# First modulations of a two-layer diffusion block: alternating weight chunks, shift from unsplit fp32 weights, and conditioning rows prepared at another place

## The chip, the cores and the metric

The kernel runs on one core of a Trainium2 chip. A core has five engines that run side by side, each with its own queue in fixed order: TensorE (PE, matmuls), VectorE (DVE), ScalarE (ACT), GpSimd (POOL) and SyncE (SP), which here only issues DMA transfers. What counts is the time of one execution on the device, in microseconds (us), lower being better.

## The reference, cut to what matters

Two layers of a block that works on 256 latent tokens beside 256 context tokens, 1024 features wide. Each layer begins with a modulation whose shift and scale come from a conditioning vector:

```python
def adaln(cond, w_ada, b_ada):
    return jnp.split(jax.nn.silu(cond) @ w_ada + b_ada, 6, axis=-1)

def modulate(x, shift, scale):
    return rms_norm(x) * (1.0 + scale) + shift

for l in range(DEPTH):
    sh1, sc1, g1, sh2, sc2, g2 = adaln(c, w_ada[l], b_ada[l])          # latent tokens
    csh1, csc1, cg1, csh2, csc2, cg2 = adaln(c_ctx, w_ada[l], b_ada[l])  # context tokens
    ... project(modulate(ctx, csh1, csc1), w_in[l])   # keys, values, gates of the context
    ... project(modulate(x, sh1, sc1), w_in[l])       # three token mixers, merged, w_o
    ... sq_relu_ffn(modulate(x_new, sh2, sc2), w_ff1[l], w_ff2[l])
```

All weights are fp32. `w_ada` is 1024 x 6144 a layer; its first 2048 columns give `sh1` and `sc1` for both conditioning vectors. They are needed before the first projection can start.

## The kernel before, in words

Tokens lie along columns, features along the 128 partitions. A precise product is made of fast passes: a weight chunk arrives as fp32 `raw` (128x1024), ScalarE rounds it to `whi`, VectorE (later in turns with POOL) forms `wlo = raw - whi`, and TensorE adds hi*hi, hi*lo and lo*hi. `emit_chunk` (L284) issues the DMA of a chunk and its split; `chunk` (L301) hands out the next chunk and emits two ahead. The order of all chunks is the list `layer_chunks`, and it begins with `START_ORDER`. Eight `raw` buffers exist at the start (four under the tag `raw`, four under `t4k`), so the DMA of chunk n + 8 waits until chunk n has been read by its split.

The start of the first layer is `start` (L1340). It runs as a main generator beside spawned chains, which a small planner (`run`) lets go on when their due time on its clock is reached (the table `LAT`); that fixes the order of TensorE and SP. The order on VectorE, ScalarE and POOL is set when the program is built. `start` does the following:

- loads `x` for both streams (`xT`, latent and context, 1 MB each), and spawns `norm_start0` (L1284) for each: squares (L1290), sums (L1294, L1295), a matmul with ones, the power -1/2 on POOL (L375), a row of 1/rms spread by two matmuls with `dg` (L519) into `Rb`, and `x*R` (L1304), one half of `x` on VectorE and one on POOL;
- computes the first modulations in four groups of 512 columns, shift and scale of the first half, then of the second (`ada_group`, L1308): the four columns of `csil` (two conditioning vectors, each as hi and lo) are the stationary operand, the split weights move, 512 columns at a time, into a `sc` bank of PSUM. `ada_rows` (L1324) turns the four rows with a small matmul against `comb` to columns and adds the bias;
- `half(i)` (L1354) makes `nt` from scale and shift for four of the eight feature blocks and splits it into `h`;
- kv and q parts of the first projection follow, four of each, `half(1)` needed by the second half of them. Then the constants are loaded (`load_constants2`, `layer_params`), the first kv and q chains are started, and last `cond_rows` (L460) prepares `sil`, the conditioning vectors in every partition, for later `ada_task` products (L490) on VectorE.

The kv chain and the q chain (`qss`, `rq`, `qt` in the rows) follow; TensorE turns `qt` and `KS` by transposes (L320), which stand among its matmuls.

Of the kernel before, what the change touches and what calls it, by code (L numbers as in the profile page):

```python
# [143 lines left out]
def shape_constants():  # L144
# [38 lines left out]
    comb = np.array([[1, 0], [0, 1], [1, 0], [0, 1]], np.float32)  # L183
# [7 lines left out]
       "ada": 1.51, "x": 0.54, "half": 1.35, "kv_lat": 6.0, "kv_ctx": 4.5, "kv_out": 0.7, "q_lat": 7.5,  # L191
# [15 lines left out]
class Builder:  # L207
# [183 lines left out]
    def load_constants(self):  # L391
# [892 lines left out]
    def norm_start0(self, s, x, R):  # L1284
# [11 lines left out]
        yield self.lat("x")  # L1296
# [5 lines left out]
        for i in range(2):  # L1302
            xh = x[:, i * 4:i * 4 + 4, :]
            (nc.vector if i == 0 else nc.gpsimd).tensor_tensor(  # L1304
                xh, xh, R.unsqueeze(1).to_broadcast([P, 4, SEQ]), op=ALU.mult)
        self.flags.add(f"R{s}")

    def ada_group(self, g):  # L1308
        c0 = ADA_START[g]
        ps = self.sc_bank()  # L1310
        for kc in range(4):
            if kc > 0:
                yield
            w = self.chunk(("B", "w_ada", c0, 512, 2 * kc))
            for kk in range(2):
                k = 2 * kc + kk
                for q in range(2):
                    self.mm(ps[:4, :], self.csil[:, k, :], w[q][:, kk * 512:(kk + 1) * 512],
                            start=(k == 0 and q == 0), stop=(k == KT - 1 and q == 1))
        rows = self.tp.tile([4, 512], F32, tag="t2k", name="adarow")  # L1320
        self.nc.scalar.copy(rows, ps[:4, :])
        self.spawn(self.ada_rows(g, rows), self.lat("ada"))

    def ada_rows(self, g, rows):  # L1324

        nc = self.nc
        out = self.sc_bank()
        ov = out[:, :8].rearrange("p (n c) -> p n c", c=2)
        for j in range(4):
            self.mm(ov[:, j, :], rows[:, j * P:(j + 1) * P], self.comb, True, True)  # L1330
# [3 lines left out]
        nc.vector.tensor_tensor(o, ov.rearrange("p n c -> p c n"), b, op=ALU.add)
        if n0 >= 8:
            nc.vector.tensor_scalar(o, o, 1.0, None, op0=ALU.add)
        self.flags.add(f"ada{g}")
        yield 0.0

    def start(self, h, kv_ready, q_ready):  # L1340
# [127 lines left out]
```

## Time and profile before

| | us |
|---|---|
| median of three runs | 1434.76 |
| fastest and slowest | 1433.84, 1438.26 |
| the profiled execution | 1438.17 |
| its span, first to last instruction | 1436.4 |
| TensorE busy | 1366.7 (95%) |
| VectorE busy | 991.7 (69%) |
| ScalarE busy | 661.6 (46%) |
| POOL busy | 451.7 (31%) |

A busy time is the sum of the times in which an engine worked on something; matmuls overlap, so a busy TensorE need not be at its peak. Wait lists name the engine and operation that released the waiting one. The mean granted TensorE clock of the span is 0.979 of full speed. The chain of work that ended last is mostly TensorE (41% of the span) and VectorE (10%).

### The profile page before, as it was taken

Reading aid. Unit: us, or ns where it says so; the run is one execution under the profiler, and the core shown is the slowest. Engines: PE = TensorE matmul, PEld = TensorE weight load, DVE = VectorE, ACT = ScalarE, POOL = GpSimd, SP = SyncE. Lnnn points to the kernel's source line nnn. Section 1 sums busy time; section 2 is a strip of 40 time slices with the busy share of each in tenths; the row PEclk is TensorE's granted clock in tenths of the full one; section 3 lists DMA queues with packets and bytes.
Section 4 is the critical chain, followed back from the end, with each engine's and each line's share of the span. In section 5 each row is a group of like instructions: output and inputs, shape, how many; then the busy total and the mean of one; then the engine's idle time right before and its main releaser. Section 6 shows DMA issues by size and latency. Waiting matters only on the chain.

```text
span 1436.4 us, 21724 instructions
## 1 busy us (share of the span) xinstructions
PE 1366.7 (95%) x8272; PEld 1192.3 (83%) x8272; DVE 991.7 (69%) x1669; ACT 661.6 (46%) x1095; POOL 451.7 (31%) x288
## 2 busy tenths in 40 slices
PE   4968998998999999999999999999999999999999
PEld 2757787877788889888887888987799999999999
DVE  7776678876576768768885566886875665864453
ACT  5755455643223335442332323555556635565443
POOL 2030002213112334553342424431110245465554
PEclk8989999998999999999999999999999999999999
DMA  7621112321354455444556656442144335556554
GB/s 301 230 73 45 59 64 68 118 103 45 118 175 162 150 196 182 158 140 172 205 207 213 216 193 215 165 149 89 48 138 149 104 118 161 180 162 202 181 178 131
DMA packets 60391, 214.08 MB, mean 149 GB/s; under 512 B 7230, under 2 KB 8510, under 8 KB 59648
## 3 DMA queue, kind: packets, MB, share of 16 engines
q1 hardware_dynamic: 58696, 209.51, 43.5%
q10 hardware_dynamic: 1592, 3.20, 0.7%
q8 instruction: 65, 1.06, 0.3%
q14 instruction: 38, 0.31, 0.1%
HBM read 211.63 MB, written 1.05 MB: 148 GB/s over the span
## 4 chain that ended last, share of the span: by engine, by line
PE 41%; DVE 10%; issue 3%; DMA 3%; ACT 1%; POOL 0%; SPq 0%; DVEq 0%; ACTq 0%; POOLq 0%
PE mm L316 37%; DVE junk L490 4%; DMA adaw<-w_adaT 3%; PE sm L316 2%; DVE wlo L298 1%; PE sc L316 1%; PE sm L320 1%; DVE acc L507 1%; ACT whi L296 0%; DVE h L546 0%; DVE x L1259 0%; DVE f L1215 0%; DVE mx L717 0%; DVE nt L541 0%; ACT gab L820 0%
## 5 line engine op out<-in xcount | busy, mean ns | idle before, releaser
L296 ACT CAST whi<-raw 128x1024 fp32r<-128x1024 f32 (+1 forms) x312 | 322.9, 1039 | 524.1 <-PE mm L316 419.0
L316 PE MATMUL mm<-h,whi 128*128 128x512 f32 (+2 forms) x2112 | 515.1, 336 | 1.7 <-ACT h L1177 0.8
L316 PEld LDWEIGHTS mm<-h,whi 128*128 128x128 f32 x2112 | 361.7, 192 | 40.8 <-DVE h L1178 1.1
L298 DVE TENSOR_TENSOR wlo<-raw,whi 128x1024 fp32r<-128x1024 f32 (+1 forms) x215 | 286.7, 1336 | 107.9 <-ACT whi L296 106.7
L316 PE MATMUL mm<-h,wlo 128*128 128x512 f32 (+2 forms) x1056 | 352.4, 334 | 0.0
L298 POOL TENSOR_TENSOR wlo<-raw,whi 128x1024 fp32r<-128x1024 f32 x97 | 240.1, 2475 | 346.7 <-ACT whi L296 340.9
L316 PE MATMUL mm<-f,whi 128*128 128x256 f32 (+1 forms) x1152 | 257.2, 319 | 0.0
L490 DVE SCALAR_TENSOR_TENSOR junk<-adaw,sil 128x1024 bf16<-128x1024 f32 x128 | 184.9, 1472 | 57.0 <-DMA adaw<-w_adaT 56.8
L316 PEld LDWEIGHTS mm<-h,wlo 128*128 128x128 f32 x1056 | 202.2, 192 | 19.2
L316 PEld LDWEIGHTS mm<-f,whi 128*128 128x128 f32 x1152 | 192.0, 191 | 15.2
L316 PE MATMUL mm<-f,wlo 128*128 128x256 f32 (+1 forms) x576 | 183.8, 319 | 2.9 <-DVE wlo L298 2.4
L316 PE MATMUL mm<-whi,h 128*128 128x512 f32 (+2 forms) x544 | 172.0, 386 | 0.0
L316 PEld LDWEIGHTS mm<-f,wlo 128*128 128x128 f32 x576 | 109.7, 190 | 11.7 <-DVE wlo L298 3.7
L316 PEld LDWEIGHTS mm<-whi,h 128*128 128x128 f32 x544 | 103.7, 199 | 16.3
L316 PE MATMUL mm<-wlo,h 128*128 128x512 f32 (+2 forms) x272 | 102.9, 378 | 0.4 <-DVE wlo L298 0.4
L1214 POOL TENSOR_TENSOR ffr<-ffr 128x512 f32<-128x512 f32 (+1 forms) x64 | 71.5, 1118 | 46.1 <-ACT f L1213 37.5
L1215 DVE TENSOR_TENSOR f<-ffr,f 128x512 fp32r<-128x512 f32 (+1 forms) x64 | 56.2, 886 | 29.7 <-POOL ffr L1214 29.5
L1259 DVE SCALAR_TENSOR_TENSOR x<-mm,ada,x 128x256 f32<-128x256 f32 x96 | 43.6, 478 | 42.5 <-PE mm L316 42.3
L383 POOL TENSOR_SCALAR gx<-gx 128x512 f32<-128x512 f32 (+1 forms) x14 | 14.0, 1000 | 183.2 <-ACT gx L382 183.1
L316 PE MATMUL mm<-m,whi 128*128 128x256 f32 x384 | 69.5, 283 | 0.0
L316 PEld LDWEIGHTS mm<-wlo,h 128*128 128x128 f32 x272 | 54.2, 199 | 8.1 <-DVE wlo L298 1.1
L1061 POOL TENSOR_TENSOR mg<-mg,gth 128x512 f32<-128x512 f32 (+1 forms) x28 | 34.4, 1230 | 84.1 <-DVE gth L1060 84.1
(291 smaller groups left out, 1828.5 us busy)
## 6 DMA issues: line engine op xcount, KB each, us to landing
raw<-wpk SPq DMA_DIRECT2D x304, 512.0 KB, 3.8
adaw<-w_adaT SPq DMA_DIRECT2D x80, 512.0 KB, 3.8
raw<-wpk SPq DMA_DIRECT2D x8, 288.0 KB, 2.9
x<-xT SPq DMA_DIRECT2D x2, 1024.0 KB, 6.9
x<-xT ACTq DMA_DIRECT2D x2, 1024.0 KB, 6.9
sil<-cond SPq DMA_DIRECT2D x1, 1024.0 KB
out<-x ACTq DMA_DIRECT2D x8, 128.0 KB, 1.7
trif<-tri SPq DMA_DIRECT2D x2, 384.0 KB, 2.9
```

Of the source, the lines that this page charges most:

```text
L296: nc.scalar.copy(hi[:, :n], raw[:, :n])
L298: eng.tensor_tensor(lo[:, :n], raw[:, :n], hi[:, :n].bitcast(F32), op=ALU.subtract)
L316: self.nc.tensor.matmul(out, lhsT, rhs, start=start, stop=stop)
L320: self.nc.tensor.transpose(out, src, self.ident)
L383: nc.gpsimd.tensor_scalar(x2[:, :n], x2[:, :n], 0.044715, 1.0, op0=ALU.mult, op1=ALU.add)
L490: nc.vector.scalar_tensor_tensor(junk, raw, 1.0, self.sil[:, c], op0=ALU.mult, op1=ALU.mult, accum_out=self.ada[l][:, c, n:n + 1])
L507: nc.vector.tensor_tensor(acc, acc, sq, op=ALU.add)
L1061: (nc.vector if m is not None and n >= KT - 2 else nc.gpsimd).tensor_tensor(mg, mg, th[:, :nt], op=ALU.add)
L1214: nc.gpsimd.tensor_tensor(r[:, :nt], r[:, :nt], r[:, :nt], op=ALU.mult)
L1215: nc.vector.tensor_tensor(lo, r[:, :nt], hi.bitcast(F32), op=ALU.subtract)
L1259: nc.vector.scalar_tensor_tensor(x[s][:, n], ps[:, s * SEQ:(s + 1) * SEQ], self.ada[l][:, s, 40 + n:41 + n], x[s][:, n], op0=ALU.mult, op1 ...
```

## The change

Sixteen chunks of `w_ada` are taken in two halves rather than four groups, shift and scale chunks alternating. Shift chunks (columns below 1024) are no longer split: TensorE reads `raw` itself, with the plain fp32 `cth` (two columns) as the stationary operand, into rows 32 and 33 of a PSUM bank. Scale chunks are split as before, into rows 0 to 3 of another. Both end in one tile `rows` of 34 partitions, which POOL sets to zero first, and `comb` grows to 34x4. The two `x` are issued among the first chunks, and `x*R` moves into `half`, all of it on VectorE. `cond_rows`, `load_constants2` and `layer_params` move ahead of the first kv part, and `cond_rows` works on pieces of 512 columns; its factor 0.5 goes into the accumulating product of `ada_task`. `comb` is loaded later. Four entries of the planner's times change (`ada`, `x`, now one for each stream, `half`, `rstd0`).

```diff
+ADA_START = ((0, 1024), (512, 1536))
-START_ORDER = [("B", "w_ada", c0, 512, kk) for c0 in ADA_START[:2] for kk in range(0, KT, 2)]
-START_ORDER += [("B", "w_ada", c0, 512, kk) for c0 in ADA_START[2:] for kk in range(0, KT, 2)]
+START_ORDER = [("B", "w_ada", c0, 512, kk) for cs in ADA_START for kk in range(0, KT, 2) for c0 in cs]
...
-       "ada": 1.51, "x": 0.54, "half": 1.35, "kv_lat": 6.0, "kv_ctx": 4.5, "kv_out": 0.7, "q_lat": 7.5,
+       "ada": 1.5, "x0": 5.0, "x1": 8.5, "half": 3.0, "kv_lat": 6.0, "kv_ctx": 4.5, "kv_out": 0.7, "q_lat": 7.5,
...
         nc.sync.dma_start(raw[:, :n], src)
+        if self.specs[i][1] == "w_ada" and self.specs[i][2] < D:
+            self.split[i] = raw, None
+            return
...
-        self.csil = self.big([P, KT, 4], F32R, name="csil")
-        self.split_hl(self.csil[:, :, 0:2], self.csil[:, :, 2:4], thv)
+        self.csil = thv
+        self.csil2 = cp.tile([P, KT, 4], F32R, name="csil2")
+        self.split_hl(self.csil2[:, :, 0:2], self.csil2[:, :, 2:4], thv)
...
         for c in range(2):
-            th = self.wp.tile([P, D], F32, tag="raw", bufs=4, name="silt")
-            nc.scalar.activation(th, self.sil[:, c], AF.Tanh, scale=0.5)
-            nc.vector.scalar_tensor_tensor(th, th, 1.0, self.sil[:, c], op0=ALU.add, op1=ALU.mult)
-            nc.vector.tensor_scalar(self.sil[:, c], th, 0.5, None, op0=ALU.mult)
+            for i in range(2):
+                v = self.sil[:, c, i * 512:(i + 1) * 512]
+                th = self.trb(name="silt")
+                nc.scalar.activation(th, v, AF.Tanh, scale=0.5)
+                nc.vector.scalar_tensor_tensor(v, th, 1.0, v, op0=ALU.add, op1=ALU.mult)
...
-        for i in range(2):
-            xh = x[:, i * 4:i * 4 + 4, :]
-            (nc.vector if i == 0 else nc.gpsimd).tensor_tensor(
-                xh, xh, R.unsqueeze(1).to_broadcast([P, 4, SEQ]), op=ALU.mult)
         self.flags.add(f"R{s}")
 
-    def ada_group(self, g):
...
+    def ada_half(self, i):
+
+        nc = self.nc
+        ps = [self.sc_bank() for _ in range(2)]
+        rows = self.tp.tile([34, 512], F32, tag="t2k", name="adarow")
+        nc.gpsimd.memset(rows, 0.0)
         for kc in range(4):
+            for j, c0 in enumerate(ADA_START[i]):
+                w, wl = self.chunk(("B", "w_ada", c0, 512, 2 * kc))
+                for kk in range(2):
+                    k = 2 * kc + kk
+                    c = slice(kk * 512, kk * 512 + 512)
+                    if j == 0:
+                        self.mm(ps[0][32:34], self.csil[:, k], w[:, c], k == 0, k == KT - 1)
+                        self.clk += 0.43
+                    else:
+                        self.mm(ps[1][:4], self.csil2[:, k], w[:, c], k == 0, False)
+                        self.mm(ps[1][:4], self.csil2[:, k], wl[:, c], False, k == KT - 1)
                 yield
+        nc.scalar.copy(rows[32:34], ps[0][32:34])
+        nc.vector.tensor_copy(rows[:4], ps[1][:4])
+        self.spawn(self.ada_rows(i, rows), self.lat("ada"))
...
         for s in range(2):
+            for _ in range(2):
+                self.emit_chunk()
             nc.sync.dma_start(x[s], self.a["xT"][s])
...
         def half(i):
-            yield from self.until(f"ada{2 * i}", f"ada{2 * i + 1}", "R0", "R1")
+            yield from self.until(f"ada{i}", "R0", "R1")
+            for s in range(2):
+                xh = x[s][:, i * 4:i * 4 + 4, :]
+                nc.vector.tensor_tensor(xh, xh, Rs[s].unsqueeze(1).to_broadcast([P, 4, SEQ]), op=ALU.mult)
...
-        self.spawn(half(0), 0.0)
-        yield from ada[2]
-        yield from ada[3]
+        for i in range(2):
+            yield from self.ada_half(i)
+            self.spawn(half(i), 0.0)
+        self.cond_rows()
+        self.load_constants2()
+        self.layer_params(0)
         yield from self.need("half0")
...
-        self.spawn(half(1), 0.0)
...
-        self.load_constants2()
-        self.layer_params(0)
...
-        self.cond_rows()
```

TensorE's first matmuls, before (a row is one instruction or several alike; outputs stand left of the arrow, `csil` and `cth` are the conditioning vectors, `dg` spreads 1/rms):

```order
L316 MATMUL sc<-whi,csil 4x512
L316 MATMUL sc<-wlo,csil 4x512
L316 MATMUL sc<-whi,csil 4x512
L316 MATMUL sc<-wlo,csil 4x512
L316 MATMUL sm<-ones,sq_126 128x1 x2
L316 MATMUL sm<-ones,sq_138 128x1 x2
```

and now:

```order
L321 MATMUL sc<-raw,cth 2x512 x2
L321 MATMUL sc<-whi,csil_105 4x512
L321 MATMUL sc<-wlo,csil_105 4x512
L321 MATMUL sc<-whi,csil_105 4x512
L321 MATMUL sc<-wlo,csil_105 4x512
L321 MATMUL sc<-raw,cth 2x512 x2
```

A shift chunk has become two fp32 matmuls in front of each scale chunk, and the statistics (`sq`) stand further back, behind the fourth chunk for the first stream.

VectorE around `x*R` (the rows `x<-x,Rb`), before:

```order
L519 TENSOR_SCALAR dg<-ident,rn 128x128 x4
L298 TENSOR_TENSOR wlo<-raw,whi 128x1024
L1304 TENSOR_TENSOR x<-x,Rb 128x1024 x2
L298 TENSOR_TENSOR wlo<-raw,whi 128x1024 x3
L1334 TENSOR_TENSOR ada_97<-sc,bada 128x2x4
L298 TENSOR_TENSOR wlo<-raw,whi 128x1024 x4
```

and now:

```order
L527 TENSOR_SCALAR dg<-ident,rn 128x128 x2
L1303 TENSOR_TENSOR sq_154<-sq_154 128x256
L303 TENSOR_TENSOR wlo<-raw,whi 128x1024 x2
L1372 TENSOR_TENSOR x<-x,Rb 128x1024 x2
L379 TENSOR_SCALAR rn<-sm 128x2
L303 TENSOR_TENSOR wlo<-raw,whi 128x1024
L1332 COPY adarow<-sc 4x512
L527 TENSOR_SCALAR dg<-ident,rn 128x128 x2
L303 TENSOR_TENSOR wlo<-raw,whi 128x1024
L1372 TENSOR_TENSOR x<-x,Rb 128x1024 x2
L1348 TENSOR_TENSOR ada_95<-sm,bada 128x2x4
```

The first halves of both `x` are scaled on VectorE, two instructions for each stream, with splits between them, and the split count ahead of `ada` is smaller.

VectorE in the first q chain (`qss` is the sum of squares of a head, `rq` its power's input, `silt` and `sil` the conditioning rows), before:

```order
L468 SCALAR_TENSOR_TENSOR silt<-silt,sil 128x1024
L627 TENSOR_TENSOR KS<-kvz,KS 128x2x64 x2
L622 TENSOR_TENSOR kvz<-kvz,parb 128x128
L469 TENSOR_SCALAR sil<-silt 128x1024
L298 TENSOR_TENSOR wlo<-raw,whi 128x1024
L665 TENSOR_REDUCE qss<-qt_701 128x8
L627 TENSOR_TENSOR KS<-kvz,KS 128x2x64 x2
L468 SCALAR_TENSOR_TENSOR silt<-silt,sil 128x1024
L374 TENSOR_SCALAR rq<-qss 128x8
```

and now:

```order
L673 TENSOR_REDUCE qss<-qt_655 128x8
L630 TENSOR_TENSOR kvz<-kvz,parb 128x128
L379 TENSOR_SCALAR rq<-qss 128x8
L303 TENSOR_TENSOR wlo<-raw,whi 128x1024
L635 TENSOR_TENSOR KS<-kvz,KS 128x2x64 x2
L676 TENSOR_TENSOR Q_119<-Q_119,rq 128x512
L303 TENSOR_TENSOR wlo<-raw,whi 128x1024
L680 TENSOR_TENSOR Q_119<-Q_119,parb 128x512
L303 TENSOR_TENSOR wlo<-raw,whi 128x1024
L685 TENSOR_TENSOR qt_655<-Q_119,qt_655 128x4x64
```

The conditioning rows are gone from here (they stand ahead of the second half's `ada` now), and two splits have come between the steps that end in `qt`.

## Rows read from the trace of the kernel before

**Rows 1.** Busy us by stretch: PE, PEld, DVE, ACT, POOL; granted clock, DMA share, GB/s

```profile
0.00:4.00 4.00, 0.00 (x0) 0.00 (x0) 1.31 (x7) 1.70 (x3) 0.70 (x6) 1.00 0.39 103
4.00:24.00 20.00, 10.07 (x37) 5.20 (x37) 14.71 (x21) 12.34 (x18) 5.47 (x4) 1.00 1.02 410
24.00:29.00 5.00, 0.17 (x1) 0.09 (x2) 5.00 (x4) 1.13 (x2) 2.56 (x1) 0.84 0.19 74
29.00:37.60 8.60, 8.60 (x25) 3.57 (x24) 5.81 (x6) 4.32 (x5) 0.00 (x0) 0.50 0.76 244
...
79.30:86.30 7.00, 0.03 (x1) 0.01 (x1) 4.91 (x9) 2.03 (x4) 4.21 (x1) 0.69 0.53 183
86.30:92.60 6.30, 6.28 (x20) 5.30 (x21) 3.81 (x11) 2.55 (x7) 1.64 (x1) 0.53 0.00 0
```

**Rows 2.** PE's waits, 0 to 132 us: total us, times, longest

```profile
PE sc L316 <- ACT whi L296: 12.8, 1, 12.8
PE sm L320 <- DVE qt L677: 7.0, 1, 7.0
PE sc L316 <- DVE wlo L298: 6.9, 4, 4.9
PE sc L316 <- ACT Pt L720: 2.6, 2, 2.4
```

**Rows 3.** Lines 1304 and 298 alone: ns min/median/max

```profile
L1304 POOL TENSOR_TENSOR x<-x,Rb x2: 2447/2886/3326, 20.8 to 23.2; 128x1024 f32<-128x1024 f32 x2
L1304 DVE TENSOR_TENSOR x<-x,Rb x2: 3360/3402/3443, 20.9 to 24.3; 128x1024 f32<-128x1024 f32 x2
...
L298 DVE TENSOR_TENSOR wlo<-raw,whi x215: 751/1224/2808, 13.1 to 1422.6; 128x1024 fp32r<-128x1024 f32 x104, 128x576 fp32r<-128x576 f32 x4
```

**Rows 4.** Timeline of PE in the first modulations: start us, us, what

```profile
30.20 1.86 PE L316 MATMUL sc<-comb,adarow 4*128 4x2 f32 x8
33.24 0.63 PE L316 MATMUL sc<-wlo,csil 128*4 128x512 f32 x1
33.66 0.63 PE L316 MATMUL sc<-whi,csil 128*4 128x512 f32 x1
...
40.06 0.40 PE L316 MATMUL sc<-wlo,csil 128*4 128x512 f32 x1
40.29 0.39 PE L316 MATMUL sc<-whi,csil 128*4 128x512 f32 x1
```

**Rows 5.** Timeline: two plain fp32 matmuls of 512 columns, as four records

```profile
257.00 1.98 PE L316 MATMUL sc<-wg,zT 33*128 33x512 f32 x4
```

**Rows 6.** Timeline of ACT: first squares of the latent stream

```profile
7.04 2.19 ACT L1290 ACTIVATE sq<-x 128x512 f32<-128x512 f32 x4 [3.14 <-DMA x<-xT]
```

**Rows 7.** Timeline of DVE and PE: first half modulated, first projection

```profile
42.48 1.38 DVE L1363 TENSOR_SCALAR nt<-x,ada 128x256 f32<-128x256 f32 x4
...
47.66 0.30 PE L316 MATMUL mm<-whi,h 128*128 128x288 f32 x1
...
48.09 1.89 DVE L368 TENSOR_TENSOR h<-nt,h 128x512 fp32r<-128x512 f32 x3
```

**Rows 8.** Timeline of PE: last of q parts, and the wait

```profile
73.50 0.39 PE L316 MATMUL sm<-whi,h 128*128 128x512 f32 x1
...
78.94 0.39 PE L316 MATMUL mm<-whi,h 128*128 128x512 f32 x1
86.32 1.94 PE L320 MATMUL sm<-ident,qt 128*128 128x128 f32 x8 [6.99 <-DVE qt L677]
```

**Rows 9.** Line 375 on POOL: ns min/median/max

```profile
L375 POOL TENSOR_TENSOR rq<-rq,mhalf x6: 1635/1734/4213, 79.6 to 969.8; 128x8 f32<-128x8 f32 x6
```

**Rows 10.** The tile silt: ns min/median/max

```profile
L467 ACT ACTIVATE silt<-sil x2: 1050/1056/1062, 72.2 to 76.3; 128x1024 f32<-128x1024 f32 x2
L468 DVE SCALAR_TENSOR_TENSOR silt<-silt,sil x2: 1220/1220/1220, 73.6 to 78.1; 128x1024 f32<-128x1024 f32 x2
L469 DVE TENSOR_SCALAR sil<-silt x2: 686/686/687, 75.4 to 80.5; 128x1024 f32<-128x1024 f32 x2
```

More of the change, by code (lines that the diff above doesn't have):

```diff
@@ L182, in shape_constants @@
     ], 1).astype(np.float32)
-    comb = np.array([[1, 0], [0, 1], [1, 0], [0, 1]], np.float32)
+    comb = np.zeros((34, 4), np.float32)
+    for r, c in ((32, 0), (33, 1), (0, 2), (1, 3), (2, 2), (3, 3)):
+        comb[r, c] = 1.0
     return {"rope": np.ascontiguousarray(rope.astype(np.float32)),
@@ L448, in cond_setup @@
         nc, cp, a = self.nc, self.cp, self.a
-        cT = self.tr(name="cT")[:, :16].rearrange("p (k c) -> p k c", c=2)
+        cT = cp.tile([P, 16], F32, name="cT").rearrange("p (k c) -> p k c", c=2)
         nc.sync.dma_start(cT, a["condT"])
-        th = self.tr(name="cth")[:, :16]
+        th = cp.tile([P, 16], F32, name="cth")
         thv = th.rearrange("p (k c) -> p k c", c=2)
@@ L456, in cond_setup @@
         nc.vector.tensor_scalar(thv, thv, 0.5, None, op0=ALU.mult)
-        self.csil = self.big([P, KT, 4], F32R, name="csil")
-        self.split_hl(self.csil[:, :, 0:2], self.csil[:, :, 2:4], thv)
+        self.csil = thv
+        self.csil2 = cp.tile([P, KT, 4], F32R, name="csil2")
+        self.split_hl(self.csil2[:, :, 0:2], self.csil2[:, :, 2:4], thv)
+        self.comb = cp.tile([34, 4], F32, name="comb")
+        nc.scalar.dma_start(self.comb, a["comb"])
     def cond_rows(self):
@@ L489, in ada_task @@
             junk = self.bp.tile([P, D], BF16, tag="b2k", name="junk")
-            nc.vector.scalar_tensor_tensor(junk, raw, 1.0, self.sil[:, c], op0=ALU.mult, op1=ALU.mult,
+            nc.vector.scalar_tensor_tensor(junk, raw, 0.5, self.sil[:, c], op0=ALU.mult, op1=ALU.mult,
                                            accum_out=self.ada[l][:, c, n:n + 1])
@@ L1295, in norm_start0 @@
         nc.vector.tensor_tensor(acc[:, :SEQ], acc[:, :SEQ], acc[:, SEQ:], op=ALU.add)
-        yield self.lat("x")
+        yield self.lat(f"x{s}")
         st = self.sm_bank()
@@ L1301, in norm_start0 @@
         nc.scalar.copy(R, R0[:, :SEQ])
-        for i in range(2):
-            xh = x[:, i * 4:i * 4 + 4, :]
-            (nc.vector if i == 0 else nc.gpsimd).tensor_tensor(
-                xh, xh, R.unsqueeze(1).to_broadcast([P, 4, SEQ]), op=ALU.mult)
         self.flags.add(f"R{s}")
-    def ada_group(self, g):
-        c0 = ADA_START[g]
-        ps = self.sc_bank()
-        for kc in range(4):
-            if kc > 0:
-                yield
[L1314 to L1322, printed above, removed]
@@ L1326, in ada_rows @@
+    def ada_rows(self, i, rows):
         nc = self.nc
-        out = self.sc_bank()
-        ov = out[:, :8].rearrange("p (n c) -> p n c", c=2)
+        out = self.sm_bank()
+        ov = out[:, :16].rearrange("p (n c) -> p n c", c=4)
         for j in range(4):
             self.mm(ov[:, j, :], rows[:, j * P:(j + 1) * P], self.comb, True, True)
-        n0 = ADA_START[g] // P
-        o = self.ada[0][:, :, n0:n0 + 4]
-        b = self.bada[:, 0, n0:n0 + 4].unsqueeze(1).to_broadcast([P, 2, 4])
@@ L1334, in ada_rows @@
[L1334 to L1337, printed above, removed]
+        for j, c0 in enumerate(ADA_START[i]):
+            n0 = c0 // P
+            o = self.ada[0][:, :, n0:n0 + 4]
+            b = self.bada[:, 0, n0:n0 + 4].unsqueeze(1).to_broadcast([P, 2, 4])
+            r = ov[:, :, 2 * j:2 * j + 2].rearrange("p n c -> p c n")
+            if j == 0:
+                nc.vector.tensor_tensor(o, r, b, op=ALU.add)
+            else:
+                nc.vector.scalar_tensor_tensor(o, r, 1.0, b, op0=ALU.add, op1=ALU.add)
@@ L1338, in ada_rows @@
+        self.flags.add(f"ada{i}")
         yield 0.0
@@ L1345, in start @@
         x = [self.big([P, KT, SEQ], name="x") for s in range(2)]
-        ada = [self.ada_group(g) for g in range(4)]
         for s in range(2):
+            for _ in range(2):
+                self.emit_chunk()
             nc.sync.dma_start(x[s], self.a["xT"][s])
@@ L1351, in start @@
         yield
-        yield from ada[0]
-        yield from ada[1]
         def half(i):
-            yield from self.until(f"ada{2 * i}", f"ada{2 * i + 1}", "R0", "R1")
+            yield from self.until(f"ada{i}", "R0", "R1")
+            for s in range(2):
+                xh = x[s][:, i * 4:i * 4 + 4, :]
+                nc.vector.tensor_tensor(xh, xh, Rs[s].unsqueeze(1).to_broadcast([P, 4, SEQ]), op=ALU.mult)
             for k in range(4 * i, 4 * i + 4):
```

6 lines of the change are left out of this document (1 added, 5 removed).

## The prediction

> **What bounds the kernel now.** I read the page first: TensorE is busy 95% of the span and the chain that ended last is mostly matmuls, but the first 90 us are its thin slices. The stretches by window show what each is limited by [rows 1]. From 4 to 24 us DMA runs full at 410 GB/s. From 24 to 29 us it drops to 74 GB/s, TensorE works 0.17 of 5 us, and VectorE is the only full engine. From 29 to 37.6 us TensorE is full, but at a granted clock of 0.50 (1.2 GHz). From 79.3 to 86.3 us it stands again, and then works 6.3 us at 0.53. The list of TensorE's waits [rows 2] names them: 12.8 us for the first split (nothing there to overlap it with), one of 4.9 us for `wlo`, 7.0 us for `qt`.
>
> The 4.9 us wait is VectorE's `x*R`: two 128x1024 products at 3.36 to 3.44 us each, beside two on POOL, while `wlo` of the same size has a median of 1.22 us [rows 3]. A split queues behind them; no buffer is given back, so DMA stops too. The clock drop that follows shows in the spacing of 512-column matmuls: 0.42 us at 33 us (33.24 to 33.66), 0.23 us at 40 us [rows 4]. So the start is bound by data first, then by VectorE's order and a slow clock. The first projection matmul (`mm`) is at 47.66, and the fourth q part ends just after 73.50 [rows 7, 8]. TensorE's order is the same in both kernels from the second `comb` product of the new one on; what changes lies before 90 us.
>
> **The change part by part.** Times below are us of the profiled span. I call the sixteen `w_ada` chunks c0 to c15; even ones are now shift, odd ones scale.
>
> *Data.* 0.41 MB are in by 4.0 us, then 0.41 MB per us [rows 1]; x0 (1.05 MB) is through at 5.6 and ScalarE's first square starts at 7.04 [rows 6], so landing takes 1.4 more. The new order c0 c1 x0 c2 c3 x1 c4 ... lands c1 at 7.0, x0 at 9.5, c3 at 12.1, x1 at 14.6, c5 at 17.2, c7 at 19.7 and c15 at 30.0. Matmuls can start at about 5.8 instead of 12.8.
>
> *TensorE.* Half of the splits go, but 16 shift matmuls are plain fp32. The only fp32 product with 512 columns shows four records for two matmuls in 1.98 us [rows 5]: 0.455 us each, 0.91 per matmul at full clock, against 2 x 0.23 for a split pair. A pair of chunks costs 1.82 + 0.92 = 2.7 us, just over the 2.55 us in which its megabyte arrives. At half clock it costs 5.4. Because TensorE is fed from 5.8 us on almost without a hole, I take it as fast from about 14 us (before, it needed 12.8 to 20.7, and 28.8 to 37.6). Cost on the path: little, as VectorE is later.
>
> *VectorE until the first projection.* Its order is the difference's second piece. The splits of c1 and c3 and the sums of x0 are done by 14.4. x1's squares end at 16.8, its sums at 17.6. POOL's first `adarow` memset stands before its power, so `dg` is done near 20.1, wlo of c5 at 21.4, of c7 at 22.6. R0 comes through TensorE behind c5 at 23.1. Then: two products x0*R 25.5, wlo of c9 (its cast is behind ScalarE's `adarow` copy) 27.3, `adarow` 27.9, `dg` 28.4, wlo c11 29.6, two products x1*R 32.0, `ada` 32.4, wlo c13 33.6, four `nt` in 1.38 [rows 7] 35.0, wlo c15 36.7, and with the first `h` parts (0.63 each) and a short wlo the kv matmuls run from 38.5. TensorE is through c15 at 37.6, so VectorE sets this.
>
> This holds if a product costs 1.22. The trace has it only at 3.40, with POOL at the same work, so the bounds are 1.22 and 3.40. I take 1.22: POOL's part is removed, and the POOL power `rq` shows the same meeting from the other side, 1.64 alone and 4.21 while VectorE ran on without a gap [rows 9]. The Trainium skill (SBUF — State Buffer, "SBUF: two separate sides") says that VectorE and GpSimd share one port pair as an exclusive lock held for a whole instruction, the loser blocking fully. By that rule each product is 1.22 and the sum is the one below; by the row alone it would be 8.7 us worse.
>
> *From there to the end of the q parts.* Before: 47.66 to 73.50, 25.8 us. Now VectorE has constants, two `ropeg`, four `sil` (0.69 each, taken from 128x512 work of that length) and `ada` ahead of the wlo of the first q chunk: it ends at 47.7, while TensorE is through with kv at 45.9. That is a new wait of 1.8 us, behind which ScalarE's casts and the second half's `nt` also queue. The second half's `h` is then in time. 38.5 + 7.4 + 1.8 + 5.4 + 6.3 + 5.2 = 64.6, against 73.50. **Term 1: -8.9 us**; bounds 0 (products at 3.40) and -12 (no new wait and handovers as short as I count).
>
> *Conditioning rows.* Gone from where they were: two ScalarE tanh of 1.05 and on VectorE 2 x (1.22 + 0.69) = 3.8 us [rows 10], all between the kv chain and `rq`, where VectorE ran without a gap. `rq` then comes earlier, but two wlo now stand between its steps, and the cast of the chunk after next cannot start before TensorE ends its last matmul at 79.3; 1.05 + 1.22 + 0.8 and handovers make a wait of at least 3.3. I take 4.0 instead of 7.0. **Term 2: -3.0 us**, bounds 0 and -3.8. The rest of the edit (0.5 moved into the accumulating product, halves instead of whole rows) costs nothing, since the tanh and products run beside kv matmuls; without that cover it is 4 x 0.69.
>
> *Clock behind that wait.* 6.3 us at half pace cost 3.1 [rows 1]. With 4 us of idling instead of 7 it may not fall. **Term 3: -1.9**, between 0 and -3.1.
>
> I keep back **1.6 us** for handovers, since the list counts engines back to back. Sum: -8.9 - 3.0 - 1.9 + 1.6 = -12.2. The profiled execution took 1438.2 (span 1436.4), so 1426.0; that execution was 3.4 above the median of 1434.8, which gives 1422.6, rounded to **1423**. Faster or slower means 0.3%, 4.3 us, about what a measurement here can tell from no change.
>
> **Rivals** (times on the median).
>
> *A, the products stay at 3.40.* VectorE gets to `nt` 8.7 us later, the first projection begins near 47 and term 1 is gone: -3.0 - 1.9 + 1.6 = -3.3, 1431.5. For it: the row is the same operation on the same operands, R being a broadcast. Against: POOL was busy with its own in all but a tenth of that time. Chance 0.10.
>
> *B, later waits take back terms 2 and 3.* TensorE's next stretch also waits, for `Pt` 2.6 us in all [rows 2], on chains of ScalarE and VectorE that the change hardly touches. Then only -8.9 + 1.6 stay: 1427.5. Chance 0.14.
>
> *C, all terms at their better bound,* -12 - 3.8 - 3.1 + 1.6 = -17: 1417.5. Chance 0.10.
>
> *D, slower: the clock stays at the lower level through the first modulations.* Its place is TensorE from 5.8 us on. Eight pairs at 5.4 us make 42.8, statistics, `dg` and `comb` at half pace 5.4 (three groups like the 1.86 of `comb` [rows 4]): the first projection starts at 54.0, and its first 8.8 us also run at half pace, as long as the second rise took, +4.4. Without the new wait the q parts end at 54.0 + 24.3 + 4.4 = 82.7, 9.2 late; less 4.9 from terms 2 and 3 that is +4.3, 1439. It decides for slower as soon as the first projection starts later than about 52. For it: the clock was at 0.50 for 8.6 us of unbroken matmuls, and matmuls with two weight columns in plain fp32 are new here. Against: those with four columns raised it twice. Chance 0.06.
>
> The Trainium skill (TensorE: Matmul & The Clock Gate, "Part 3: Packing small matmuls") holds that matmuls whose outputs lie in different 32-row groups of PSUM run side by side. Shift (rows 32, 33) and scale (0 to 3) would then overlap; D's 42.8 us would shrink to 29 and D would not be slower. No row here shows such an overlap; it is one reason for D's small chance, and it would leave the sum alone, where VectorE is later.
>
> **How the numbers follow.** Forecast 0.60, A 0.10, B 0.14, C 0.10, D 0.06. All of the forecast, B and C are under 1430.5, and about a third of A: 0.86 faster. The rest of A and some of D are within: 0.10; slower 0.04. The range goes from C's 1417.5, less 2 for the spread of single executions, to A's 1431.5: 1415 to 1432, leaving out D and little else.
>
> **What would show it.** Right: `x*R` near 1.22 us on VectorE; no DMA gap at 24 to 29 us; 512-column fp32 matmuls as two records 0.455 us apart; first `mm` near 38 to 40; the `qt` wait 3.3 to 5 us. Wrong: first `mm` after 45 (A or D, told apart by the length of `x*R` and the spacing of `sc` matmuls); a wait over 3 us before the first q chunk, which would mean that `sil` landed late; a `qt` wait still near 7.

## The result and the profile after

| | kernel before | changed kernel |
|---|---|---|
| median, us | 1436.51 (1433.84 to 1439.18, 4 runs) | 1420.39 (1419.07 to 1423.01, 4 runs) |
| ratio, 95% interval | | 0.9899 [0.9881, 0.9918] |
| profiled execution, its span | 1438.17, 1436.4 | 1419.23, 1417.4 |
| mean granted clock of that execution | 0.979 | 0.984 |

The change made the kernel 1.0% faster, 16.1 us on the medians; 1423 had been forecast, in a range from 1415 to 1432. The profiled pair lies 18.9 us apart.

The stretches by window of the changed kernel (columns as in [rows 1]) show what became of the start:

```profile
0.00:4.00 4.00, 0.00 (x0) 0.00 (x0) 1.29 (x7) 1.71 (x3) 0.70 (x6) 1.00 0.50 122
4.00:24.00 20.00, 16.53 (x45) 4.08 (x46) 12.57 (x19) 10.45 (x15) 1.95 (x3) 0.91 1.02 415
24.00:29.00 5.00, 4.36 (x21) 2.00 (x20) 4.85 (x7) 2.48 (x4) 0.95 (x2) 1.00 1.02 405
29.00:36.00 7.00, 7.00 (x20) 1.20 (x18) 6.34 (x12) 6.03 (x11) 0.00 (x0) 1.00 1.04 399
```

DMA has no hole at 24 us any more (405 GB/s instead of 74), TensorE works 4.36 of those 5 us instead of 0.17, and from 29 us it runs at a granted clock of 1.00 instead of 0.50 [rows 1]. TensorE's timeline has the first modulations and the first projection (`mm`), VectorE's the products and the first `h`:

```profile
5.15 3.44 PE L321 MATMUL sc<-raw,cth 128*2 128x512 f32 x4 [5.15 <-DMA raw<-wpk]
...
15.18 3.54 PE L321 MATMUL sc<-raw,cth 128*2 128x512 f32 x4
...
31.74 1.88 PE L321 MATMUL sc<-raw,cth 128*2 128x512 f32 x4
33.55 0.40 PE L321 MATMUL sc<-whi,csil 128*4 128x512 f32 x1
...
37.07 0.40 PE L321 MATMUL sc<-wlo,csil 128*4 128x512 f32 x1
37.31 0.29 PE L321 MATMUL mm<-whi,h 128*128 128x288 f32 x1
```

```profile
21.28 2.35 DVE L1372 TENSOR_TENSOR x<-x,Rb 128x1024 f32<-128x1024 f32 x2
...
27.43 2.36 DVE L1372 TENSOR_TENSOR x<-x,Rb 128x1024 f32<-128x1024 f32 x2
...
34.16 0.68 DVE L373 TENSOR_TENSOR h<-nt,h 128x512 fp32r<-128x512 f32 x1
```

The first projection starts at 37.31 instead of 47.66 [rows 7], with no wait noted: TensorE comes straight from the last scale matmul, while VectorE had the first `h` by 34.8. The four products are both halves of the latent stream's `x` (from 21.28) and then both of the context stream's (from 27.43), so VectorE has none left for the second half. The second part of the gain is in the list of waits to 132 us (total us, times, longest) and in the timeline around `qt`:

```profile
PE sc L321 <- DMA raw<-wpk: 5.7, 2, 5.2
PE sm L325 <- DVE zT L649: 3.4, 2, 1.8
PE sm L325 <- DVE qt L685: 2.7, 1, 2.7
```

```profile
67.58 0.39 PE L321 MATMUL mm<-whi,h 128*128 128x512 f32 x1
68.01 1.04 ACT L301 CAST whi<-raw 128x1024 fp32r<-128x1024 f32 x1 [1.66 <-PE mm L321]
69.09 1.23 DVE L303 TENSOR_TENSOR wlo<-raw,whi 128x1024 fp32r<-128x1024 f32 x1 [0.88 <-ACT whi L301]
...
70.23 0.76 DVE L685 TENSOR_TENSOR qt<-Q,qt 128x256 f32<-128x256 f32 x2
70.70 1.09 PE L325 MATMUL sm<-ident,qt 128*128 128x128 f32 x8 [2.73 <-DVE qt L685]
...
71.55 0.48 PE L321 MATMUL mm<-whi,h 128*128 128x512 f32 x1
...
71.87 0.39 PE L321 MATMUL mm<-wlo,h 128*128 128x512 f32 x1
...
76.94 0.66 PE L325 MATMUL sm<-ident,KS 128*128 128x128 f32 x4 [1.83 <-DVE zT L649]
```

The wait for `qt` is 2.73 us instead of 6.99 [rows 2, 8], made of three steps in a row: the cast, `wlo`, and the first of the two pieces of `qt`. Behind it the transposes take 1.09 instead of 1.94 us, so the clock did not fall. A new wait of 1.83 us for `zT` gives a little back, and a later one of 2.1 us for `lsum`, which the kernel before has at 109 us, is gone. Start times of the same matmul in the two traces differ by 10.4 us at the first `mm`, 15.6 at the `qt` transposes, about 18 at 115 us and 18.9 at the end.

Part of this is clock. By windows, ahead of and behind 200 us, before first and then after:

```profile
0.00:200.00 200.00, 161.56 (x791) 122.13 (x791) 139.17 (x324) 111.26 (x233) 26.13 (x22) 0.92 0.37 133
200.00:1440.00 1240.00, 1205.12 (x7483) 1070.18 (x7481) 852.58 (x1346) 550.35 (x862) 425.53 (x266) 0.99 0.46 151
```

```profile
0.00:200.00 200.00, 177.83 (x874) 129.57 (x875) 142.49 (x351) 113.66 (x248) 19.26 (x24) 0.97 0.38 140
200.00:1440.00 1240.00, 1186.58 (x7384) 1055.29 (x7382) 839.74 (x1313) 540.05 (x839) 426.30 (x264) 0.99 0.46 150
```

In steps of 2 us, the first 200 us hold 30.7 us at the lower level (1.2 GHz) before and 13.6 after; behind them it is 32.0 and 32.2 ("low clock" from here on). These sums leave out the very first matmuls: the clock column reads 1.00 there, yet the first shift chunk above took 3.44 us, and a later one 1.88; in the kernel before, the first matmuls too ran 0.43 us apart instead of 0.23, up to 20.7 us.

### The profile page after: what moved, and what is told of

Its sections match the earlier page's. It is cut to its first block, busy times and chain, and to the rows that moved or that the text cites. A ratio compares the mean times of both kernels' runs of the same rounds, so it can differ in the third digit from the quotient of the medians.

```text
span 1417.4 us, 21658 instructions
## 1 busy us (share of the span) xinstructions
PE 1364.4 (96%) x8256; PEld 1184.9 (84%) x8256; DVE 982.2 (69%) x1663; ACT 653.7 (46%) x1087; POOL 445.6 (31%) x288
## 4 chain that ended last, share of the span: by engine, by line
PE 42%; DVE 10%; DMA 3%; issue 3%; ACT 1%; POOL 0%; SPq 0%; DVEq 0%; ACTq 0%; POOLq 0%
PE mm L321 38%; DVE junk L498 5%; DMA adaw<-w_adaT 3%; DVE wlo L303 2%; PE sm L321 2%; PE sc L321 1%; PE sm L325 1%; DVE acc L515 1%; ACT whi L301 0%; DVE h L554 0%; DVE x L1267 0%; DVE mx L725 0%; DVE f L1223 0%; DVE nt L549 0%; ACT gab L828 0%
## 5 line engine op out<-in xcount | busy, mean ns | idle before, releaser
L301 ACT CAST whi<-raw 128x1024 fp32r<-128x1024 f32 (+1 forms) x304 | 314.9, 1039 | 514.6 <-PE mm L321 410.3
L303 DVE TENSOR_TENSOR wlo<-raw,whi 128x1024 fp32r<-128x1024 f32 (+1 forms) x207 | 275.3, 1331 | 111.6 <-ACT whi L301 110.7
L498 DVE SCALAR_TENSOR_TENSOR junk<-adaw,sil 128x1024 bf16<-128x1024 f32 x128 | 196.7, 1564 | 56.8 <-DMA adaw<-w_adaT 56.7
L321 PEld LDWEIGHTS mm<-whi,h 128*128 128x128 f32 x544 | 102.4, 196 | 15.6
L1223 DVE TENSOR_TENSOR f<-ffr,f 128x512 fp32r<-128x512 f32 (+1 forms) x64 | 49.5, 783 | 27.1 <-POOL ffr L1222 26.9
L321 PEld LDWEIGHTS mm<-m,whi 128*128 128x128 f32 x384 | 59.9, 192 | 0.1
```

The lines of the kernel that those rows point to most:

```text
L321: self.nc.tensor.matmul(out, lhsT, rhs, start=start, stop=stop)
L498: nc.vector.scalar_tensor_tensor(junk, raw, 0.5, self.sil[:, c], op0=ALU.mult, op1=ALU.mult, accum_out=self.ada[l][:, c, n:n + 1])
L1223: nc.vector.tensor_tensor(lo, r[:, :nt], hi.bitcast(F32), op=ALU.subtract)
```

## The experiments

Every ratio is to runs of the kernel before made beside the edited one (medians 1434.5 to 1437.2, so differences of 2 us between two edited kernels are not told apart). One tool is used below. Over all 191 runs of the thirteen kernels whose clock is known, a run is 1.21 us longer than another run of the same kernel for each 0.001 by which its mean granted clock is lower; what is left scatters by 1.2 us. So each kernel's mean time can be taken to one clock, 0.982, and a difference split into clock and the rest. It is an estimate: an edit that moves the clock does part of its work in the other column.

| first modulations | rows early | x\*R on VectorE | median, us | mean clock | at 0.982 |
|---|---|---|---|---|---|
| old (the kernel before, 80 runs) | no | no | 1436.6 | 0.9804 | 1434.1 |
| old | yes | no | 1436.1 | 0.9786 | 1432.1 |
| old | no | yes | 1435.4 | 0.9804 | 1433.8 |
| old | yes | yes | 1426.7 | 0.9835 | 1428.7 |
| new | no | no | 1434.4 | 0.9792 | 1430.6 |
| new | yes | no | 1420.5 | 0.9843 | 1424.2 |
| new | no | yes | 1423.7 | 0.9845 | 1426.4 |
| new (the change, 10 runs) | yes | yes | 1420.4 | 0.9846 | 1423.9 |

### Undoing one small part of the change

Conditioning rows late again:

```diff
-        self.cond_rows()
         self.load_constants2()
...
         q_ready((yield from self.proj_b("w_in", C_QB, 512, h, [0, 1])))
+        self.cond_rows()
```

> The changed kernel with one part undone: the conditioning rows (sil) are prepared at their old place, after the last q part, still in pieces of 512 columns. Theory (terms 2 and 3 are real): first kv matmul unchanged near 37.3 us, end of the fourth q part about 1 us earlier than 62.2 because nothing stands ahead of the first q chunk's wlo, then the wait for qt back from 2.7 to 6 to 7 us with a clock fall behind it; 4 to 6 us slower than the changed kernel. Rival (later waits take such gains back): the qt wait grows as well, but the difference is gone by 130 us of the span and the time is within 1.5 us of the changed kernel.

1423.66 us (6 runs), ratio to before 0.9911 [0.9891, 0.9930]: 3.3 above the changed kernel, between theory and rival. Its wait for `qt` is back:

```profile
75.38 1.97 PE L325 MATMUL sm<-ident,qt 128*128 128x128 f32 x8 [6.29 <-DVE qt L685]
```

The products shared with POOL again:

```diff
+        for i in range(2):
+            xh = x[:, i * 4:i * 4 + 4, :]
+            (nc.vector if i == 0 else nc.gpsimd).tensor_tensor(
+                xh, xh, R.unsqueeze(1).to_broadcast([P, 4, SEQ]), op=ALU.mult)
...
-            for s in range(2):
-                xh = x[s][:, i * 4:i * 4 + 4, :]
-                nc.vector.tensor_tensor(xh, xh, Rs[s].unsqueeze(1).to_broadcast([P, 4, SEQ]), op=ALU.mult)
```

> The changed kernel with x*R as before: straight after R, first half on VectorE and second half on POOL. Theory (VectorE and POOL hold each other up where both read SBUF): VectorE's products measure 3.3 to 3.5 us instead of 1.2, but there are two instead of four, so VectorE loses about 2 us before the first h; as TensorE now runs through to the first kv matmul without a wait, at most 1.5 us of that shows: 0 to +1.5 us. Rival (a product with R broadcast has 3.4 of its own and something else made it 1.2): products stay at 1.2 and the time is the same or up to 1 us better, with two products less on VectorE.

1420.52 (6 runs), ratio 0.9897 [0.9875, 0.9918]: the same as the changed kernel, as both expectations allowed. VectorE's products took 1.23, which the theory had missed (3.3 to 3.5); it was POOL's that took longer. The timeline is the cleanest view of how VectorE and POOL meet:

```profile
21.32 1.23 DVE L1312 TENSOR_TENSOR x<-x,Rb 128x1024 f32<-128x1024 f32 x1
21.37 3.40 POOL L1312 TENSOR_TENSOR x<-x,Rb 128x1024 f32<-128x1024 f32 x1 [4.43 <-ACT Rb L1309]
...
28.92 3.40 POOL L1312 TENSOR_TENSOR x<-x,Rb 128x1024 f32<-128x1024 f32 x1 [3.02 <-ACT Rb L1309]
...
30.28 3.15 DVE L1381 TENSOR_SCALAR nt<-x,ada 128x256 f32<-128x256 f32 x4
```

and the first of these four alone:

```profile
30.28 2.18 DVE L1381 TENSOR_SCALAR nt<-x,ada 128x256 f32<-128x256 f32 x1
```

VectorE's product, 0.05 us ahead, takes 1.23 beside POOL's; POOL's 3.40 is that 1.23 and another 2.17, a little under the 2.45 of POOL's product that started first in the kernel before [rows 3]. The first `nt` (0.40 each elsewhere) takes 2.18 and ends 0.14 us behind POOL's second product. So of such a pair whichever starts first runs at its own pace, and the other ends after it. In the kernel before POOL was 0.1 us ahead [rows 3], and both products of VectorE, with the splits queued behind them, ended after POOL's. The Trainium skill (SBUF — State Buffer, "SBUF: two separate sides") states such a rule: the two engines share a port pair that the first to start holds for its whole instruction. The rows agree.

Both undone at once, the new first modulations alone (edits as above; the constants and the planner's times stay as the change has them, and no run undid these by themselves):

> Both smaller parts of the change undone at once: conditioning rows late again, and x*R split between VectorE and POOL again. What is left is the new first modulations alone. Theory (the parts add up: late rows cost 3.3, the POOL products nothing measurable): 1423 to 1425.5, about 12 under the kernel before. Rival (the parts need each other, the POOL products now meet the splits as before): first mm at 42 or later and 1428 or more.

1434.41 (12 runs), ratio 0.9982 [0.9961, 1.0002]. The theory that parts add up failed by 10 us, and so did the rival's reason, though not its time: the first `mm` came at 39.78, not at 42 or later. The front of its trace is 9.9 us ahead of before at 200 us, but only 3.2 at 400 and 2.0 at the end, with 47 us at the lower clock behind 200 us against 32:

```profile
0.00:200.00 200.00, 172.40 (x827) 124.92 (x828) 134.79 (x332) 107.03 (x234) 26.03 (x24) 0.95 0.36 133
200.00:1440.00 1240.00, 1201.93 (x7431) 1068.31 (x7429) 846.79 (x1330) 546.54 (x853) 424.46 (x266) 0.98 0.46 151
```

### Doing one small part on the kernel before

Rows early:

```diff
         yield from ada[3]
+        self.cond_rows()          # with its body as in the change
...
-        self.cond_rows()
```

> The kernel before with one part of the change alone: conditioning rows prepared ahead of the first kv part, in pieces of 512 columns, factor 0.5 in the accumulating product. Theory: the qt wait of 7.0 us shrinks to 2.5 to 4.5 and the clock behind it mostly stays up; the first kv matmul stays near 47.7; 1 to 2 us are lost ahead of the second half's h; 4 to 6 us faster than before. Rival (later waits take it back): within 1.5 us of before.

1436.08 (12 runs), ratio 1.0000 [0.9985, 1.0015]. The theory failed, though its mechanism worked: the wait for `qt` went from 6.99 to 2.82, and the trace was 9.5 us ahead from 115 to 200 us. It was 5.9 ahead at 350 us and 0.9 at the end, again with more low clock behind 200 us (47.6 us).

```profile
PE sm L320 <- DVE qt L678: 2.8, 1, 2.8
```

All of x\*R on VectorE:

```diff
-            (nc.vector if i == 0 else nc.gpsimd).tensor_tensor(
+            nc.vector.tensor_tensor(
```

> The kernel before with one edit: all four x*R products on VectorE, none on POOL, same place. Theory (they hold each other up): each product 1.2 us, four take 4.9 instead of 6.7 for two, the wait for wlo at 24 to 29 us shrinks from 4.9 to about 3, and if the clock stays up the following modulations also run at 0.23 us a matmul: 1.5 to 6 us faster. Rival (3.4 is the product's own price): four take 13.6 us, the wait grows to 11 to 12 us and the time is 6 to 8 us worse.

1435.43 (12 runs, 1427.66 to 1440.84), ratio 1.0000 [0.9985, 1.0015]: no gain that shows, though the theory's mechanism worked. Four products took 4.62 us on VectorE instead of two in 6.72, the first `mm` came at 41.81, and the longest wait for `wlo` was 1.4 instead of 4.9.

```profile
20.92 4.62 DVE L1304 TENSOR_TENSOR x<-x,Rb 128x1024 f32<-128x1024 f32 x4
```

The profiled execution was the fastest of the twelve by 6 us, with 10.2 us of low clock in the first 200 us and 25.3 behind them; the others left no trace, so it says nothing on where they lost it.

Both together:

> The kernel before with both smaller parts of the change, and its first modulations as they were: conditioning rows early, all of x*R on VectorE. Alone they gave 1.2 and 1.8 us, within the noise. Theory (each saves work, but most of what their traces gain by 130 us, 8 to 10 us, goes again in more low clock): first mm at 40 to 42, wait for qt 2.8, 1429 to 1435. Rival (the two need each other, since the new first modulations without them gave only 2.3 of 16): 1422 to 1427, most of the gain of the change.

1426.69 (12 runs), ratio 0.9935 [0.9914, 0.9955]. The theory had the first `mm` (41.42) and the wait for `qt` right and missed the time. The rival came out: the two need each other. They give 9.6 us, most of the change on the medians, and about half of it at equal clock (5.4 of 10.2). Here both early waits are short, and the first 200 us hold 10.3 us of low clock instead of 30.7:

```profile
PE sc L316 <- DVE wlo L298: 3.5, 4, 1.4
PE sm L320 <- DVE qt L678: 2.8, 1, 2.8
```

### The first modulations

Shift chunks split like the scale chunks, with TensorE's order of chunks kept (`adarow` becomes two tiles of four rows, and `comb` is as in the kernel before):

```diff
-        if self.specs[i][1] == "w_ada" and self.specs[i][2] < D:
-            self.split[i] = raw, None
-            return
...
-                        self.mm(ps[0][32:34], self.csil[:, k], w[:, c], k == 0, k == KT - 1)
+                    self.mm(ps[j][:4], self.csil2[:, k], w[:, c], k == 0, False)
+                    self.mm(ps[j][:4], self.csil2[:, k], wl[:, c], False, k == KT - 1)
```

> Alternating chunks stay, but the shift chunks are split again like the scale ones (eight more casts on ScalarE, eight more wlo on VectorE, TensorE 0.93 instead of 1.81 us a shift chunk). Theory (unsplit shift takes work off VectorE, which has no room for it): VectorE was busy 23.8 of the 32 us from 4 to 36 us; 8 x 1.22 = 9.8 more make 33.6, so VectorE becomes the bound, the first mm comes at 39 to 41 us instead of 37.3 and the time is 1422 to 1426. Rival (TensorE is the only bound of the new start, unsplit shift costs 8 x 0.88 = 7 us on it): first mm at 33 to 35.5, 1416 to 1418.

1428.88 (12 runs), ratio 0.9957 [0.9934, 0.9980]: the theory's direction, with more loss than it gave. The first `mm` is 8.4 us later than in the changed kernel. Behind the first wait of 6.7 us, which stands where the changed kernel waits 5.2 for data, TensorE waits 3.1 us more for casts and 5.2 for `wlo`:

```profile
PE sc L316 <- ACT whi L296: 9.8, 4, 6.7
PE sc L316 <- DVE wlo L298: 5.2, 5, 1.5
```

```profile
45.73 0.45 PE L316 MATMUL mm<-whi,h 128*128 128x288 f32 x1
```

So unsplit shift is what makes the new first modulations pay: with split shift they are not clearly better than the old ones with the same two small parts (1428.88 against 1426.69 above, 1426.8 against 1428.7 at equal clock). Of the 8.5 us that unsplit shift gives on the medians, 2.9 are left at equal clock. By an estimate from single rows, unsplit shift takes 9.8 us (8 x 1.22) from VectorE and eight casts from ScalarE, and costs TensorE 7 us more (8 x 0.88).

Both `x` first:

```diff
         for s in range(2):
-            for _ in range(2):
-                self.emit_chunk()
             nc.sync.dma_start(x[s], self.a["xT"][s])
```

> Both x are issued ahead of the chunks, as in the kernel before; all else as after. The first chunk then lands some 5 us later. Theory (TensorE has some 5 us of waits and 1.7 us of slow clock among the first chunks, part of which it gets back): first matmul at 10 to 11, first mm at 38 to 41, 1421.5 to 1424.5. Rival (what TensorE does first is all that counts): first mm at 42 or later, 1425 or more.

1423.41 (6 runs), ratio 0.9908 [0.9881, 0.9936], 3.0 above the changed kernel, as the theory had it, but within the scatter (the means differ by 1.8 us). The first matmul came at 10.51, the first `mm` at 39.03. Of 5.4 us lost at the front TensorE got back 3.6, against the trace above.

No chunk split at all:

```diff
-        if self.specs[i][1] == "w_ada" and self.specs[i][2] < D:
+        if self.specs[i][1] == "w_ada":
...
-                        self.mm(ps[1][:4], self.csil2[:, k], w[:, c], k == 0, False)
-                        self.mm(ps[1][:4], self.csil2[:, k], wl[:, c], False, k == KT - 1)
+                        self.mm(ps[1][:2], self.csil[:, k], w[:, c], k == 0, k == KT - 1)
+                        self.clk += 0.43
...
-        nc.vector.tensor_copy(rows[:4], ps[1][:4])
+        nc.vector.tensor_copy(rows[:2], ps[1][:2])
```

> Scale chunks are not split either: plain fp32 on TensorE, no casts and no wlo for the first modulations. Theory (TensorE sets the first mm): a pair of chunks costs 3.6 instead of 2.75 us, 8 x 0.9 = 7 more, less some 2 of waits for whi and wlo that go: first mm at 41 to 43, 1424 to 1427. Rival (VectorE's list or the transfers set it, as the prediction had it): VectorE loses 9.8 us of work, first mm at 37.3 to 39, 1419.5 to 1422.

1422.58 (6 runs, 1413.97 to 1424.81), ratio 0.9895 [0.9863, 0.9927]. The theory failed: the first `mm` came at 35.73, earlier than in the changed kernel and than the rival had it (37.3 to 39). TensorE's timeline shows why (PEld is its weight load):

```profile
13.20 3.71 PE L321 MATMUL sc<-raw,cth 128*2 128x512 f32 x8
...
15.03 0.09 PEld L321 LDWEIGHTS sc<-raw,cth 128*2 128x2 f32 x2 [0.89 <-DMA raw<-wpk]
...
18.32 1.89 PE L321 MATMUL sc<-raw,cth 128*2 128x512 f32 x8
...
22.51 1.89 PE L321 MATMUL sc<-raw,cth 128*2 128x512 f32 x8
...
27.07 8.72 PE L321 MATMUL sc<-raw,cth 128*2 128x512 f32 x28
35.73 0.40 PE L321 MATMUL mm<-whi,h 128*128 128x288 f32 x1
```

A plain fp32 matmul leaves two records. Eight records, four matmuls, take 3.71 us one after the other where the second chunk came late (its weight load waits for DMA until 15.03), and 1.89 where a shift and a scale chunk were both there: the records of shift and scale then start 0.01 to 0.02 us apart. Whether that hangs on the rows was the next question; the scale product in rows 32 and 33 of its bank, like shift in its own (against the run of unsplit chunks; the copy to `adarow` reads these rows):

```diff
-                        self.mm(ps[1][:2], self.csil[:, k], w[:, c], k == 0, k == KT - 1)
+                        self.mm(ps[1][32:34], self.csil[:, k], w[:, c], k == 0, k == KT - 1)
```

> All chunks unsplit as in the run before it, but the scale product goes to rows 32 and 33 of its bank, the rows that shift uses in its own bank, instead of rows 0 and 1. Theory (plain fp32 products of shift and scale ran side by side because their outputs lie in other rows): they go one after the other again, a pair of chunks costs 3.6 instead of 1.8 us, first mm at 41 to 44, 1425 to 1430. Rival (it is the different banks, or plain fp32 itself): first mm at 35 to 37, 1421 to 1424.

1430.32 (12 runs), ratio 0.9972 [0.9950, 0.9995]: 7.7 us slower by this edit alone, the theory's side, with the first `mm` at 45.46, 1.5 us later than it said. Eight records take 3.60 us again, and a stretch of 28 takes 12.18, where the unsplit run needed 8.72 for as many (some of that at the lower clock):

```profile
28.84 3.60 PE L321 MATMUL sc<-raw,cth 128*2 128x512 f32 x8
...
33.35 12.18 PE L321 MATMUL sc<-raw,cth 128*2 128x512 f32 x28
```

So these plain fp32 matmuls run side by side when their outputs lie in rows 32 and 33 and in rows 0 and 1, and not when they lie in the same rows of two banks. The Trainium skill (TensorE: Matmul & The Clock Gate, "Part 3: Packing small matmuls") states that small matmuls run concurrently in one array at different tile positions, the column of which goes by where the output starts in PSUM (row 0, 32, 64 or 96). The rows of these two runs agree. In the changed kernel shift (plain fp32) and scale (split) use different rows too, and do not overlap: shift at 31.74, scale at 33.55. What keeps them apart was not tried.

TensorE in the run of unsplit chunks still waited 1.7 us for the `adarow` copy, queued on VectorE behind x\*R, and 1.7 for `dg`:

```profile
PE sm L321 <- DVE adarow L1332: 1.7, 1, 1.7
PE sm L321 <- DVE dg L527: 1.7, 1, 1.7
```

Hence a version of it with both copies on ScalarE, and without the extra planner time of the scale products:

```diff
-        nc.vector.tensor_copy(rows[:2], ps[1][:2])
+        nc.scalar.copy(rows[:2], ps[1][:2])
...
-                        self.clk += 0.43          # behind the scale product
```

> All chunks unsplit, scale in rows 0 and 1 again; both copies to adarow on ScalarE, which idles there, and the planner's clock for the scale products at its plain value. In the run of all unsplit chunks TensorE waited 1.7 us for VectorE's adarow copy (behind x*R) and 1.7 for dg. Theory (these waits set the first mm): it comes at 32.5 to 34.5 and the time is 1417 to 1421, below the changed kernel. Rival (the last landing, h or the clock takes it back): first mm at 35.5 or later, 1421 to 1425.

1416.36 (1415.64 to 1419.39, 5 runs), ratio 0.9871 [0.9842, 0.9899]. The first `mm`, at 33.62, came as the theory had it, and the time is 0.6 us under its range.

```profile
26.05 7.03 PE L321 MATMUL sc<-raw,cth 128*2 128x512 f32 x28
...
33.62 0.40 PE L321 MATMUL mm<-whi,h 128*128 128x288 f32 x1 [0.54 <-ACT whi L301]
```

To set the two side by side, the changed kernel ran once more:

> The changed kernel once more, unedited, since it has only four times so far and the comparisons of 2 to 6 us lean on them. Theory (its gain is stable, and all unsplit chunks with the copies on ScalarE are better still): 1419 to 1422.5, most runs above the 1415.6 to 1419.4 of that kernel. Rival (the four runs were high, the two kernels are the same): median at 1416 to 1418.

1420.74 (1418.30 to 1423.07, 6 runs), ratio 0.9905 [0.9885, 0.9925]: in the theory's range, though only three of the six runs lie above those of the version without splits. Over its ten runs the median is 1420.4, so the version without splits is the faster one by about 4 us on the medians, 3.0 at equal clock; the intervals of the two ratios still overlap. This second trace of the changed kernel also shows how far two executions of one program differ: the first `mm` comes at 38.08 instead of 37.31, and behind 200 us it has 25.1 us of low clock instead of 32.2.

## Why the prediction came out right, step by step

- **Data, and plain fp32 matmuls:** right. Matmuls start at 5.15 (5.8), shift costs 1.81 a chunk at full clock, and DMA does not pause before 36 us.
- **The products at 1.22, against 3.40:** right, 1.22 each (two in 2.35), and rival A is out. The run with POOL back showed the reason and a limit: with the rows early it costs nothing to share the products again (1420.52), since VectorE has no split waiting beside POOL's first product. With the rows late it costs 10.8 us (1423.66 to 1434.41), of which the traces show 2.0 by 200 us (11.9 against 9.9 ahead of the kernel before); the rest comes later.
- **TensorE fast from about 14 us:** wrong in both directions. It was fast from 8.5 us already (matmuls 0.23 us apart), but the clock fell once more at 15 us, and the shift chunk at 15.18 took 3.54 instead of 1.88 us.
- **VectorE sets the first projection at 38.5:** wrong in what sets it, near in time. TensorE did, at 37.31, where the prediction had it through at 37.6; VectorE had the first `h` 2.5 us earlier. Its list ran some 2 us ahead of the predicted one from the first products on, which ended at 23.63 instead of 25.5. That the time came out near is in part luck: the prediction had the two engines 0.9 us apart there, and the one that it had as the earlier set the time.
- **A new wait of 1.8 us ahead of the first q part:** did not appear. TensorE reached that part at 44.87, and `wlo` landed in time.
- **Term 1, -8.9:** measured about -11.4, from the last q part at 62.15 against 73.50; the bound of -12 assumed just what happened, no new wait and short handovers.
- **Term 2, -3.0:** measured -4.3, beyond its bound of -3.8. The step that failed is "at least 3.3": it counted both pieces of `qt`, but the transposes start behind the first.
- **Term 3, -1.9:** with 2.7 us of idling the clock stayed up, and the gain was nearly the whole 3.1. The 1.8 us for `zT` took part of that back, as rival B had it in kind, at another place and smaller.
- **The sum:** -12.2 forecast; -16.1 and -13.8 (1434.50 to 1420.74) on the medians, and -18.9 between the two profiled executions, to which the terms refer. Each term was too small, and the 1.6 us kept back were not needed: 11.4, 4.3 and 3.1 make 18.8, and the new waits (`zT`) and those gone (`lsum`) about cancel. The forecast of 1423 came nearer than its terms also by luck: it starts from 1434.8, the median of three runs; from 1436.6, the median of 80, the same sum gives 1424.4. 1420.4 lies about midway between the forecast and rival C's 1417.5. D did not come true: the clock rose early and fell once in the first modulations, instead of staying low.
- **The adding itself** is what the experiments put in doubt. The terms were added as if each held alone, and none of the three parts alone gives more than 2.3 us (table). At equal clock the three give 2.0, 0.3 and 3.5 apart, and 10.2 together. The prediction counted clock in one term and one place; of 16.2 us between the pooled medians (15.3 between the means), some 5 (0.0042 at 1.21 per 0.001) are a higher mean clock.

What stays open is why one part alone gains so little. Two of the three traces with one part only have more low clock behind 200 us, where the program is the same (47 us against 32), and lose there most of what they had gained. The third, a run far faster than its fellows, has 25.3. A single trace cannot settle it, since two traces of the changed kernel differ by 7 us in the same place. What all runs say is in the table: with one part only the mean clock is no higher than in the kernel before (0.9786, 0.9804 and 0.9792 against 0.9804). The cause is not shown.

## What to carry to other kernels

Read a short wait together with the granted clock behind it, and expect that removing one of several early waits may show nothing while removing two does, as it was here: test parts in pairs before dropping one as worthless. When many runs exist, plot time against mean clock within each kernel, then compare kernels at one clock. Work moved off a crowded engine can be paid for on TensorE at a discount, if plain fp32 products with few output rows are put into different groups of rows (1422.58 against 1430.32 us here).

## What the hardware showed beyond expectation

- Plain fp32 products of a 512-column operand with two weight columns, outputs in rows 32 and 33 and in rows 0 and 1: four in 1.89 us; with both in rows 32 and 33 of two banks, 3.60.
- A VectorE product 0.05 us ahead of POOL's ran in 1.23 us; POOL's then took 3.40, against 2.45 where POOL started first [rows 3].
- The same program ran from 1428.05 to 1442.85 us in 80 runs, with mean clocks from 0.976 to 0.986.
